# Gate table by adding DMAs, without a one-hot stage, and 96 blocks of the first expert product computed ahead and kept in DRAM

## The chip, the core and the metric

The kernel runs on one core of a Trainium2 chip. The metric is device time in microseconds (us) for one execution. The engines are TensorE (PE; PEld is its weight load), VectorE (DVE), ScalarE (ACT), GpSimd (POOL) and SyncE (SP). SP and ACT issue plain DMAs; GpSimd issues the indirect ones, whose addresses come from a list of indices in SBUF. All of them run on the core's 16 DMA engines.

## The reference

One layer of an encoder serves 512 prompt tokens and 128 sample tokens. Everything up to the last sub-layer (projection, gating, two attentions, delta rule, output projection, norms) is untouched by the change, except that zeros are written to DRAM meanwhile. The last sub-layer retrieves experts by product keys:

```python
q = (h @ w_query).reshape(n, PEER_HEADS, 2, PEER_DQ // 2)
s = jnp.einsum('nhpd,hpkd->nhpk', q, sub_keys, preferred_element_type=jnp.float32)
top_s, top_i = lax.top_k(s, PEER_TOPK)
cand = top_s[:, :, 0, :, None] + top_s[:, :, 1, None, :]
best_s, best_c = lax.top_k(cand.reshape(n, PEER_HEADS, PEER_TOPK * PEER_TOPK), PEER_TOPK)
...
ids = (i1 * PEER_NKEYS + i2).reshape(n, PEER_HEADS * PEER_TOPK)
gates = jax.nn.softmax(best_s, axis=-1).reshape(n, PEER_HEADS * PEER_TOPK)
act = jax.nn.gelu(jnp.einsum('nkd,nd->nk', expert_u[ids], h))
return jnp.einsum('nk,nkd->nd', (gates * act).astype(h.dtype), expert_v[ids])
```

There are 8 heads, 128 keys in each half, 16 picks per head, so 128 (expert, gate) pairs per token out of 128 x 128 = 16384 experts of width 1024.

## The kernel before, in words

Tokens are handled in five tiles of 128 (tiles 0 to 3 prompt, 4 sample). Tiles 0 to 2 (384 tokens, `ND`) take the dense way: for each of 128 blocks of 128 experts the first product (`u_block`, 24 matmuls: high and low parts of a split float32, 8 depth slices) gives 128 experts x 384 tokens, GELU (`u_gelu`) follows, the result is multiplied by a dense table of gates (`g_hi`), split again, and the second product (`v_bank`, 18 matmuls in six accumulators) adds it to the output. Tiles 3 and 4 take the sparse way: for each of their 128 picks, `tick` has GpSimd gather 128 rows of 4 KB of `u` or of `v` by index, and `consume` has VectorE make a dot product (pass 0) or a scaled accumulation (pass 1); that is 2 tiles x 2 passes x 128 = 512 gathers of 512 KB, with six row buffers.

The order of the stages is this. `d_prompt` computes queries and scores of the prompt tiles, 16 half heads one after the other; VectorE picks the top 16 of 128 keys (`half`, `top16`) and of the 80 candidate pairs (`best`). `d_sample` computes the scores of the sample tile. `d_decode` turns picks into expert numbers and gates, tile by tile. `table` makes the dense gates: for each token two one-hot rows (first key; second key times gate), 128 x 128 matmuls, evictions into `stg`, and 12 stores of 2 MB to the DRAM table `gdense`. Beside these, `prefill` computes the first 8 (`LEAD`) blocks of the first product. Up to here a scheduler orders each engine's queue by program order and readiness; `lanes` only interleaves the generators by their yields.

The last loop (`for m in range(NBLK)`, 128 iterations) is ordered by hand: iteration m issues the loads of later blocks on SP (`u_load`, `v_load`, every fourth time `gt_load`, one slice of the gate table), splits block m + 1 of `v` and of the gated activations, splits block m + `LEAD` + 1 of `u`, computes block m + `LEAD` of the first product and block m of the second, and in four places runs `tick` up to `goal(m)`, so that gathers are spread to iteration 118 (`END`). The sample tile's own selection (`sample_select`) lies in iterations 0 to 23. `u_split` and `split` are a cast on ScalarE and a subtraction on VectorE or GpSimd.

Of the kernel before, what the change touches and what calls it, by code (L numbers as in the profile page):

```python
# [14 lines left out]
BF16 = mybir.dt.bfloat16  # L15
# [7 lines left out]
P = 128  # L23
# [5 lines left out]
LEAD = 8  # L29
# [140 lines left out]
def body(tc, I, O):  # L170
# [498 lines left out]
    for i, job in enumerate(jobs):  # L669
        fetch(i + 2)  # L670
        w = ready[i]
# [633 lines left out]
    i1f = T(gq, [P, 4, P], "i1f")  # L1305
    i2f = T(gq, [P, 4, P], "i2f")
    iob = T(gq, [P, 16, 8], "iob", BF16)
    dx = ExitStack()
    qp = pool(dx, "qp", bufs=2, side="right")
    keysT = T(qp, [P, 16, P], "keysT", bufs=1)  # L1310
    V.tensor_copy(out=iob, in_=C("iota")[:, 0:16].unsqueeze(2).to_broadcast([P, 16, 8]))
    LOW = -3.0e38
# [10 lines left out]
    class Select:  # L1323
# [17 lines left out]
        def best(self, h):  # L1341
# [3 lines left out]
            V.tensor_copy(out=self.tib[:, :, :, :, h], in_=self.ti)  # L1345
            cand = T(self.p, [P, nt, 80], "cand", bufs=1)
# [6 lines left out]
            for t in range(nt):  # L1353
                top16(self.p, self.bs[:, t, h, :], self.bc[:, t, h, :], cand[:, t, :], 80, "rest2")
                yield t
# [43 lines left out]
    sel = Select(qp, 4, lambda: T(qp, [P, 16, 16, 8], "eq", BF16, bufs=1))  # L1399
# [12 lines left out]
    def d_prompt():  # L1412
# [28 lines left out]
        for j in range(17):  # L1441
# [12 lines left out]
            if pend is not None:  # L1454
                scores(*pend)
                yield 0.9
# [52 lines left out]
    def d_decode():  # L1509
        for t in range(4):  # L1510
            for cost in sel.decode(t, gates[:, t, :], i1f[:, t, :], i2f[:, t, :]):
                yield 7 if cost is None else 0
        V.scalar_tensor_tensor(out=i1f[:, 3, :], in0=i1f[:, 3, :], scalar=128.0, in1=i2f[:, 3, :], op0=ALU.mult, op1=ALU.add)
        V.tensor_copy(out=idq, in_=i1f[:, 3, :])

    idq = T(gq, [P, P], "idq", U32)

# [14 lines left out]
    def u_block(n):  # L1532

        u = uhs.pop(n)
        gas[n] = T(eu, [P, ND], "ga", bufs=LEAD + 1)
# [7 lines left out]

    def u_gelu(n, pa):
        S.activation(gas[n], pa[:, 0:ND], AF.Gelu_apprx_tanh)

    uls, uhs, gas = {}, {}, {}

    def prefill():
        uls[0] = u_load(0)  # L1550
        uls[1] = u_load(1)
        uhs[0] = u_split(uls.pop(0), G)
        yield 0
        for n in range(LEAD):
            uls[n + 2] = u_load(n + 2)
            uhs[n + 1] = u_split(uls.pop(n + 1), G)
# [9 lines left out]
    gd_ = T(dp, [NG, P, 12, 4, 32], "gdense")  # L1566
    gts = {}

    def gt_load(g):
        gts[g] = T(ep, [P, 12, 4, 32], "gt2") if g % 2 else T(rw, [P, 12, 4, 32], "gt")  # L1570
        nc.sync.dma_start(out=gts[g], in_=gd_[g])

    tx = ExitStack()
    tp = pool(tx, "tp", bufs=2, side="right")

    iob8 = T(tp, [P, P, 8], "iob8", BF16, bufs=1)
    V.tensor_copy(out=iob8, in_=C("iota").unsqueeze(2).to_broadcast([P, P, 8]))

    POOLS = (6, 5, 6, 5)

    def table():
        for t in range(3):
            pt = bank("tp")
            for k, src in enumerate((i1f, i2f, gates)):
                transpose(pt[:, k * P:(k + 1) * P], src[:, t, :])
            sm = T(tp, [P, 2, P], "slots")
            i1b = T(tp, [P, P], "i1b", BF16)
            S.copy(out=i1b, in_=pt[:, 0:P])
            S.copy(out=sm.rearrange("p k t -> p (k t)"), in_=pt[:, P:384])
            iot = C("iota").unsqueeze(1).to_broadcast([P, 8, P])  # L1590

            def slot(k, c, n):
                return sm[:, k, c:c + n].unsqueeze(2).to_broadcast([P, n, P])

            for c in range(4):
                stg = T(tp, [P, P, 32], "stg")
                for n0 in range(0, 32, 8):
                    col = 32 * c + n0
                    ob = T(tp, [P, P, 8], "ob", BF16, bufs=2)
                    o1 = T(tp, [P, 8, P], "o1", bufs=3)  # L1600
                    o2 = T(tp, [P, 8, P], "o2", bufs=3)
                    V.tensor_tensor(out=ob, in0=iob8, in1=i1b[:, col:col + 8].unsqueeze(1).to_broadcast([P, P, 8]), op=ALU.is_equal)  # L1602
                    obn = ob.rearrange("p e n -> p n e")
                    m = POOLS[(col // 8) % 4]
                    G.tensor_tensor(out=o1[:, 0:m, :], in0=obn[:, 0:m, :], in1=slot(1, col, m), op=ALU.mult)  # L1605
                    for n in range(m, 8):
                        S.activation(o1[:, n, :], obn[:, n, :], AF.Copy, scale=sm[:, 1, col + n:col + n + 1])
                    V.tensor_tensor(out=o2, in0=iot, in1=slot(0, col, 8), op=ALU.is_equal)
                    for q in range(0, 8, 4):
# [263 lines left out]
```

## Time and profile before

| what | value |
|---|---|
| three runs | 2171.67, 2174.33 and 2174.74 us, median 2174.33 |
| the profiled execution | 2175.44 us |
| its span, first to last instruction | 2173.7 us |
| mean granted TensorE clock | 0.958 |
| instructions | 32417 |
| DMA traffic | 575.8 MB, of it 268.47 MB by GpSimd's gathers |

The profile counts an engine as busy while an instruction runs on it; durations overlap at their ends, so the distance from start to start is the better price of an instruction in a row of its like. "Idle before" is the time an engine stood still ahead of an instruction, with what released it; "issue" means that nothing in the profile released it. PEclk is the granted clock as a share of the full 2.4 GHz. DMA is the mean busy share of the 16 DMA engines.

### The profile page before, as it was taken

Reading aid. Unit: us, or ns where it says so; the run is one execution under the profiler, and the core shown is the slowest. Engines: PE = TensorE matmul, PEld = TensorE weight load, DVE = VectorE, ACT = ScalarE, POOL = GpSimd, SP = SyncE. Lnnn points to the kernel's source line nnn. Section 1 sums busy time; section 2 is a strip of 40 time slices with the busy share of each in tenths; the row PEclk is TensorE's granted clock in tenths of the full one; section 3 lists DMA queues with packets and bytes.
Section 4 is the critical chain, followed back from the end, with each engine's and each line's share of the span. In section 5 each row is a group of like instructions: output and inputs, shape, how many; then the busy total and the mean of one; then the engine's idle time right before and its main releaser. Section 6 shows DMA issues by size and latency. Waiting matters only on the chain.

```text
span 2173.7 us, 32417 instructions
## 1 busy us (share of the span) xinstructions
PE 1914.0 (88%) x11971; PEld 1603.3 (74%) x11971; DVE 1795.8 (83%) x3883; ACT 726.1 (33%) x1220; POOL 935.3 (43%) x693
## 2 busy tenths in 40 slices
PE   5889899999889887767779999999999999999983
PEld 3889766645667776656668888888888888888862
DVE  5762367766478999968999999999999999999987
ACT  3322133312332338862233333333333332333320
POOL 1322221101312248742346666665666665565610
PEclk8999999999999999998899999999999999999996
DMA  7212242166663436566779999999999999999961
GB/s 273 111 44 79 103 143 103 40 237 227 254 217 137 157 105 181 168 191 243 249 276 409 409 390 390 398 398 398 395 410 405 380 407 383 398 386 404 388 244 68
DMA packets 200248, 575.80 MB, mean 265 GB/s; under 512 B 20463, under 2 KB 73199, under 8 KB 195226
## 3 DMA queue, kind: packets, MB, share of 16 engines
q1 hardware_dynamic: 117978, 295.59, 37.2%
q0 software_dynamic: 73728, 268.47, 31.8%
q10 hardware_dynamic: 8384, 9.68, 1.3%
q8 instruction: 94, 1.54, 0.3%
q14 instruction: 64, 0.52, 0.1%
HBM read 538.79 MB, written 34.36 MB: 264 GB/s over the span
## 4 chain that ended last, share of the span: by engine, by line
issue 17%; POOL 16%; DVE 14%; DMA 5%; ACT 2%; PE 1%; POOLq 0%; ACTq 0%; DVEq 0%
POOL acc L1653 8%; POOL rows L1653 8%; DVE ycs L1668 2%; ACT uh L243 2%; DVE vl L1698 1%; DVE rows L1662 1%; DVE acc L1668 1%; DVE acc L1662 1%; DMA acc<-in_v_dram,idq 1%; DVE ul L244 1%; DMA acc<-in_v_dram,ids 1%; DVE ga L1702 1%; DMA rows<-in_v_dram,idq 1%; DVE wl L1708 1%; DMA acc<-in_u_dram,ids 1%
## 5 line engine op out<-in xcount | busy, mean ns | idle before, releaser
L1705 ACT CAST wh<-ga 128x384 fp32r<-128x384 f32 x128 | 65.7, 514 | 764.0 <-DVE ga L1702 764.0
L188 PE MATMUL mm<-h2h,uh 128*128 128x384 f32 x1024 | 213.8, 350 | 46.6 <-ACT uh L243 45.7
L188 PEld LDWEIGHTS mm<-h2h,uh 128*128 128x128 f32 x1024 | 183.8, 194 | 73.2 <-ACT uh L243 66.3
L188 PE MATMUL mm<-h2l,uh 128*128 128x384 f32 x1024 | 204.6, 341 | 0.0
L188 PE MATMUL mm<-h2h,ul 128*128 128x384 f32 x1024 | 200.6, 336 | 0.0
L188 PE MATMUL sa<-vl,wh 128*128 128x512 f32 x384 | 161.5, 421 | 28.0 <-DVE vl L1698 28.0
L188 PEld LDWEIGHTS mm<-h2l,uh 128*128 128x128 f32 x1024 | 184.2, 193 | 0.0
L188 PE MATMUL sa<-vh,wh 128*128 128x512 f32 x384 | 153.7, 400 | 33.7 <-ACT wh L1705 30.0
L244 DVE TENSOR_TENSOR ul<-ur,uh 128x1024 fp32r<-128x1024 f32 x119 | 145.8, 1226 | 44.2 <-ACT uh L243 44.0
L188 PEld LDWEIGHTS mm<-h2h,ul 128*128 128x128 f32 x1024 | 180.5, 189 | 0.0
L1698 DVE TENSOR_TENSOR vl<-vr,vh 128x1024 fp32r<-128x1024 f32 x128 | 156.1, 1219 | 20.8 <-ACT vh L1695 20.8
L188 PE MATMUL sa<-vh,wl 128*128 128x512 f32 x384 | 152.3, 397 | 0.0
L188 PE MATMUL sa<-o,o 128*128 128x128 f32 x768 | 109.1, 292 | 47.4 <-ACT stg L1613 27.6
L1695 ACT CAST vh<-vr 128x1024 fp32r<-128x1024 f32 x128 | 133.3, 1041 | 39.1 <-DVE vr L1693 21.5
L188 PEld LDWEIGHTS sa<-o,o 128*128 128x128 f32 x768 | 95.8, 198 | 60.8 <-ACT stg L1613 33.5
L243 ACT CAST uh<-ur 128x1024 fp32r<-128x1024 f32 x128 | 134.0, 1047 | 6.9 <-PE mm L188 5.4
L1605 POOL TENSOR_TENSOR o<-ob,slots 128x768 f32<-128x768 bf16 (+1 forms) x48 | 114.5, 2392 | 32.1 <-DVE ob L1602 28.5
L1653 POOL DMA_INDIRECT acc<-in_u_dram,idq x65 | 80.1, 1232 | 109.0 <-DVE gates L1662 101.7
L188 PEld LDWEIGHTS sa<-vl,wh 128*128 128x128 f32 x384 | 73.4, 191 | 67.9 <-DVE vl L1698 54.9
L1653 POOL DMA_INDIRECT rows<-in_u_dram,idq x63 | 80.4, 1277 | 72.4 <-DVE gates L1662 67.1
L244 POOL TENSOR_TENSOR wlo<-raw,whi 128x2048 fp32r<-128x2048 f32 (+1 forms) x12 | 55.2, 4603 | 126.1 <-ACT whi L243 123.3
L188 PEld LDWEIGHTS sa<-vh,wh 128*128 128x128 f32 x384 | 73.1, 190 | 47.6 <-ACT wh L1705 32.6
(482 smaller groups left out, 4849.0 us busy)
## 6 DMA issues: line engine op xcount, KB each, us to landing
ur<-in_uT_dram SPq DMA_DIRECT2D x128, 512.0 KB
vr<-in_v_dram SPq DMA_DIRECT2D x128, 512.0 KB
gt<-gdense SPq DMA_DIRECT2D x32, 768.0 KB
gdense<-stg SPq DMA_DIRECT2D x11, 2048.0 KB
wada<-in_wada_dram SPq DMA_DIRECT2D x16, 1024.0 KB
acc<-in_ckT_dram SPq DMA_DIRECT2D x32, 512.0 KB
cv<-in_cv_dram SPq DMA_DIRECT2D x32, 512.0 KB
wqr<-in_wq_dram SPq DMA_DIRECT2D x32, 512.0 KB
```

Of the source, the lines that this page charges most:

```text
L188: PE.matmul(out, lhsT=lhsT, rhs=rhs, start=start, stop=stop, **kw)
L243: S.copy(out=hi, in_=raw)
L244: e_lo.tensor_tensor(out=lo, in0=raw, in1=hi.bitcast(F32), op=ALU.subtract)
L1605: G.tensor_tensor(out=o1[:, 0:m, :], in0=obn[:, 0:m, :], in1=slot(1, col, m), op=ALU.mult)
L1653: G.indirect_dma_start(out=r, out_offset=None, in_=I["v"] if k else I["u"], in_offset=bass.IndirectOffsetOnAxis(ap=who[t][0][:, s:s + 1], ...
L1662: V.tensor_tensor_reduce(out=r, in0=r, in1=h2, scale=1.0, scalar=0.0, op0=ALU.mult, op1=ALU.add, accum_out=act[:, s:s + 1])
L1668: V.scalar_tensor_tensor(out=facc[t], in0=r, scalar=act[:, s:s + 1], in1=facc[t], op0=ALU.mult, op1=ALU.add)
L1695: S.copy(out=vs[n][0], in_=w)
L1698: V.tensor_tensor(out=vs[n][1], in0=vls.pop(n), in1=vs[n][0].bitcast(F32), op=ALU.subtract)
L1702: V.tensor_tensor(out=ga.rearrange("p (c n) -> p c n", c=12), in0=ga.rearrange("p (c n) -> p c n", c=12), in1=gts[n // 4][:, :, n % 4, :], ...
L1705: S.copy(out=ws[n][0], in_=ga)
L1708: V.tensor_tensor(out=ws[n][1], in0=gas.pop(n), in1=ws[n][0].bitcast(F32), op=ALU.subtract)
```

## The change

The one-hot stage goes. Instead the gates are placed by address. In the early projection stage SP writes zeros over a DRAM table `gsc` of 128 x 128 x 384 floats, in 16 DMAs. `SelectHead.best` decodes each head as soon as its picks are known, for four tiles at once, and computes for tiles 0 to 2 the flat address expert x 384 + token in `idx`. `add_gates` then issues, for one tile and one of the 128 picks, an indirect DMA of 128 single floats that adds the gates to the table; 3 x 128 = 384 of them. They are issued by GpSimd: nine after each half head's scores, three at a time in `d_add` beside the sample's scores, the rest in a new loop. Adds of the same tile and different heads may meet at one element and are ordered; all others are declared free of each other.

The new loop, ordered by hand, computes blocks 5 to 95 (`FIRST`) of the first product alone; `prefill` does blocks 0 to 4. Their GELUs go to the DRAM tensor `gad` by ACT's queue. In it run the remaining adds, 170 (`EARLY_ROWS`) of the 512 gathers, and one step of `sample_select` per block; an add with no gather behind it is followed by a one-element memset. The last loop reads the blocks below 96 back (`ga_load`), and computes first-product blocks only from iteration 90 on; `LEAD` is 6, the loads run three blocks ahead, and the table slices are read from `gsc`. The low parts of the first blocks of `u` are made by VectorE instead of GpSimd.

```diff
-LEAD = 8
+LEAD = 6
+FIRST = 96
...
+    gsc = T(dp, [P * P * ND, 1], "gsc")
+    zero = T(rg, [P, 768], "zero", bufs=1)
+    G.memset(zero, 0.0)
+    def gates_zero(i):
+        a = P * ND // 16
+        nc.sync.dma_start(out=gsc.rearrange("(p x) one -> p (x one)", p=P)[:, i * a:(i + 1) * a].rearrange("p (r z) -> p r z", z=768),
+                          in_=zero.unsqueeze(1).to_broadcast([P, a // 768, 768]))
...
+        for k in range(2 if i in (1, 2, 3, 4, 5, 6, 7, 8) else 0):
+            gates_zero(2 * (i - 1) + k)
...
+    class SelectHead(Select):
+        def __init__(self, pl):
+            self.p, self.nt = pl, 4
+        def best(self, h):
+            pl, tv = self.p, self.tv
+            tib = T(pl, [P, 16, 2, 4], "tib", BF16)
+            V.tensor_copy(out=tib.rearrange("p n k t -> p t k n"), in_=self.ti)
+            bs = T(pl, [P, 4, 16], "bs")
...
+            hs = slice(16 * h, 16 * h + 16)
+            e = T(pl, [P, 4, 16], "e")
+            V.tensor_tensor(out=e, in0=bs, in1=bs[:, :, 0:1].to_broadcast([P, 4, 16]), op=ALU.subtract)
+            S.activation(e, e, AF.Exp)
...
+            ku = T(pl, [P, 4, 16], "ku", U32)
+            V.tensor_scalar(out=ku, in0=bc, scalar1=3, scalar2=None, op0=ALU.logical_shift_right)
+            kf, pf, y = (T(pl, [P, 4, 16], n) for n in ("kf", "pf", "yk"))
...
+            eq = T(pl, [P, 16, 16, 8], "eq", BF16, bufs=1)
+            V.tensor_tensor(out=eq, in0=ab_.unsqueeze(2).to_broadcast([P, 16, 16, 8]),
+                            in1=iob.unsqueeze(1).to_broadcast([P, 16, 16, 8]), op=ALU.is_equal)
+            V.tensor_tensor(out=eq, in0=eq, in1=tib.rearrange("p n k t -> p n (k t)").unsqueeze(1).to_broadcast([P, 16, 16, 8]), op=ALU.mult)
+            for n in (8, 4, 2):
+                V.tensor_tensor(out=eq[:, :, 0:n, :], in0=eq[:, :, 0:n, :], in1=eq[:, :, n:2 * n, :], op=ALU.add)
+            i12 = T(pl, [P, 16, 8], "i12")
+            V.tensor_tensor(out=i12, in0=eq[:, :, 0, :], in1=eq[:, :, 1, :], op=ALU.add)
+            ids_ = T(pl, [P, 4, 16], "idf")
+            i12v = i12.rearrange("p s (k t) -> p k t s", k=2)
+            V.scalar_tensor_tensor(out=ids_, in0=i12v[:, 0], scalar=128.0, in1=i12v[:, 1], op0=ALU.mult, op1=ALU.add)
+            V.tensor_copy(out=idq[:, hs], in_=ids_[:, 3, :])
+            V.scalar_tensor_tensor(out=idx[:, :, hs], in0=ids_[:, 0:3, :], scalar=float(ND),
+                                   in1=pnt.unsqueeze(2).to_broadcast([P, 3, 16]), op0=ALU.mult, op1=ALU.add)
+            to_add.extend((t, h, r) for t in range(3) for r in range(16))
+            yield
...
+    sel = SelectHead(qp)
+    to_add = []
+    def add_gates(n):
+        for _ in range(min(n, len(to_add))):
+            t, h, r = to_add.pop(0)
+            c = 16 * h + r
+            ins = G.indirect_dma_start(out=gsc, out_offset=bass.IndirectOffsetOnAxis(ap=idx[:, t, c:c + 1], axis=0),
+                                       in_=gates[:, t, c:c + 1], in_offset=None, compute_op=ALU.add).ins
+            for key in [f"add{t}_{h}"] + [f"add{u}" for u in range(3) if u != t]:
+                tc.declare_no_dep(ins, group=key, reason="no element in common")
+            for key in (f"add{t}_{h}", f"add{t}"):
+                tc.add_to_no_dep_group(key, ins)
...
                 scores(*pend)
+                add_gates(9)
...
-    def d_decode():
-        for t in range(4):
-            for cost in sel.decode(t, gates[:, t, :], i1f[:, t, :], i2f[:, t, :]):
-                yield 7 if cost is None else 0
...
+    gad = T(dp, [FIRST, P, ND], "gad")
...
+            S.activation(fresh[n], pa[:, 0:ND], AF.Gelu_apprx_tanh)
+            nc.scalar.dma_start(out=gad[n], in_=fresh.pop(n))
...
+    EARLIEST = 5
...
+        for n in range(EARLIEST):
+            uls[n + 3] = u_load(n + 3)
+            uhs[n + 1] = u_split(uls.pop(n + 1), V)
             u_gelu(n, u_block(n))
-            yield 5
-    gen_u = prefill()
-    lanes((d_sample(), 0, 1.0), (d_decode(), 0, 1.0), (itertools.islice(gen_u, 3), 0, 1.0))
+            yield 6
...
+    def d_add():
+        while to_add:
+            add_gates(3)
+            yield 1.9
+    lanes((d_sample(), 0, 1.0), (prefill(), 0, 1.0), (itertools.islice(d_add(), 16), 0, 1.0))
...
-    def table():
-        for t in range(3):
...
+        nc.sync.dma_start(out=gts[g], in_=gsc.rearrange("(g b e n) one -> g e b (n one)", b=4, e=P, n=ND)[g])
...
+    def ga_load(n):
+        if n < FIRST:
+            gas[n] = T(ep, [P, ND], "gr", bufs=3)
+            nc.sync.dma_start(out=gas[n], in_=gad[n])
+    EARLY_ROWS = 170
 
     def goal(m):
-        cost = lambda n: 2 * min(n, NBLK - LEAD) + max(0, n - (NBLK - LEAD))
-        return int(len(work) * min(1.0, cost(m + 1) / cost(END)))
+        cost = lambda n: n + max(0, n - (FIRST - LEAD)) - max(0, n - (NBLK - LEAD))
+        return EARLY_ROWS + int((len(work) - EARLY_ROWS) * min(1.0, cost(m + 1) / cost(END)))
...
+    for n in range(EARLIEST, FIRST):
+        left = FIRST - 3 - n
+        k = n - EARLIEST
+        to = EARLY_ROWS * (k + 1) // (FIRST - EARLIEST)
+        if n + 3 < NBLK:
+            uls[n + 3] = u_load(n + 3)
+        if n == FIRST - 2:
+            for b in range(2):
+                v_load(b)
+                ga_load(b)
+        quota = -(-len(to_add) // left) if left > 0 else len(to_add)
+        for q in range(quota):
+            add_gates(1)
+            if at[0] < to:
+                tick(at[0] + 1)
+            else:
+                G.memset(spare, 0.0)
+            if q == 0:
+                uhs[n + 1] = u_split(uls.pop(n + 1), V)
+        if not quota:
+            uhs[n + 1] = u_split(uls.pop(n + 1), V)
+        tick(to)
+        u_gelu(n, u_block(n))
+        for _ in itertools.islice(ssel, 1):
+            pass
+    for _ in ssel:
+        pass
+    gt_load(0)
+    v_load(2)
+    ga_load(2)
...
+    FIN = NBLK - LEAD - 1
     for m in range(NBLK):
-        n = m + LEAD
-        g0 = goal(m - 1) if m else 0
+        n = m + LEAD if m + LEAD >= FIRST else NBLK
+        g0 = goal(m - 1) if m else EARLY_ROWS
         part = lambda j: tick(g0 + (goal(m) - g0) * j // 4)
-        if n + 2 < NBLK:
-            uls[n + 2] = u_load(n + 2)
-        if m + 2 < NBLK:
-            v_load(m + 2)
+        if n + 3 < NBLK:
+            uls[n + 3] = u_load(n + 3)
+        if m + 3 < NBLK:
+            v_load(m + 3)
+            ga_load(m + 3)
...
```

## Rows read from the trace of the kernel before

**Rows 1.** The page: busy time by engine; DMA share in 40 slices.
```profile
PE 1914.0 (88%) x11971; PEld 1603.3 (74%) x11971; DVE 1795.8 (83%) x3883; ACT 726.1 (33%) x1220; POOL 935.3 (43%) x693
...
DMA  7212242166663436566779999999999999999961
```

**Rows 2.** Windows: us, busy of each engine (instructions), granted clock, DMA share, GB/s.
```profile
560.00:751.00 191.00, 172.89 (x1243) 138.95 (x1234) 150.37 (x898) 58.51 (x96) 49.07 (x24) 0.97 0.53 191
751.00:803.00 52.00, 45.18 (x301) 42.44 (x300) 50.56 (x120) 18.20 (x42) 12.96 (x5) 0.93 0.35 122
803.00:965.00 162.00, 114.55 (x802) 101.17 (x801) 155.97 (x96) 140.39 (x220) 124.58 (x55) 0.97 0.57 163
965.00:1126.00 161.00, 111.04 (x480) 97.41 (x479) 135.02 (x381) 36.12 (x50) 48.22 (x41) 0.86 0.73 251
1126.00:2068.00 942.00, 907.12 (x4462) 792.70 (x4462) 892.71 (x1102) 298.68 (x430) 579.46 (x460) 1.00 1.01 396
2068.00:2174.00 106.00, 64.09 (x243) 49.66 (x241) 88.04 (x168) 16.89 (x24) 7.44 (x6) 0.77 0.41 148
```

**Rows 3.** Timeline of TensorE, one iteration: start, us, instruction, count.
```profile
1241.08 0.40 PE L188 MATMUL sa<-vh,wh 128*128 128x512 f32 x1
...
1245.22 1.55 PE L188 MATMUL mm<-h2h,uh 128*128 128x384 f32 x8
...
1249.38 0.40 PE L188 MATMUL sa<-vh,wh 128*128 128x512 f32 x1
```

**Rows 4.** Timeline of VectorE, same iteration and a later one; [idle before].
```profile
1238.59 1.22 DVE L1662 CUSTOM_DVE_ANT_0 acc<-acc,h2q 128x1024 f32<-128x1024 f32 x1
...
1239.74 0.55 DVE L1702 TENSOR_TENSOR ga<-ga,gt 128x384 f32<-128x384 f32 x1
1241.36 0.08 DVE L1662 DVE_READ_ACCUMULATOR2_ANT gates<- 128x1 f32 x1
1241.82 1.23 DVE L244 TENSOR_TENSOR ul<-ur,uh 128x1024 fp32r<-128x1024 f32 x1 [0.39 <-ACT uh L243]
...
1482.84 1.23 DVE L244 TENSOR_TENSOR ul<-ur,uh 128x1024 fp32r<-128x1024 f32 x1 [0.32 <-ACT uh L243]
```

**Rows 5.** The page's costliest groups: busy, mean ns, idle before: the one-hot rows.
```profile
L1605 POOL TENSOR_TENSOR o<-ob,slots 128x768 f32<-128x768 bf16 (+1 forms) x48 | 114.5, 2392 | 32.1 <-DVE ob L1602 28.5
```

**Rows 6.** Groups by shape; one source line (min/median/max ns, first, last start).
```profile
L1316 DVE MAX8 tv<-sc 128x8 f32<-128x128 f32 x64 | 16.8, 281 | 32.8 <-ACT sc L1425 32.8
...
L244 POOL TENSOR_TENSOR wql<-wqr,wqh 128x1024 fp32r<-128x1024 f32 x16 | 38.3, 2394 | 102.4 <-PE mm L188 57.3 <-ACT wqh L243 30.7 <-PE sa L188 14.4
...
L1345 DVE CAST tib<-ti x8: 447/453/457, 595.6 to 748.2; 128x128 bf16<-128x128 uint32 x8
```

**Rows 7.** GpSimd's gathers: the source line's forms, then four instructions of its timeline.
```profile
L1653 POOLq EVENT_SEMAPHORE  x503: 17/17/43, 798.2 to 2076.7; - x168
L1653 POOL DMA_INDIRECT acc<-in_u_dram,idq x65: 937/1015/1967, 802.7 to 1290.3; - x65
...
817.80 1.25 POOL L1653 DMA_INDIRECT acc<-in_u_dram,idq  x1 [0.16 <-issue]
...
1238.94 1.68 POOL L1653 DMA_INDIRECT acc<-in_u_dram,idq  x1 [0.60 <-DVE gates L1662]
1240.93 1.31 POOL L1653 DMA_INDIRECT acc<-in_u_dram,idq  x1 [0.30 <-issue]
...
1482.51 0.94 POOL L1653 DMA_INDIRECT rows<-in_v_dram,idq  x1 [0.30 <-issue]
```

**Rows 8.** DMA: GpSimd's queue (packets, MB, share); a window of the one-hot stage.
```profile
q0 software_dynamic: 73728, 268.47, 31.8%
...
850.00:950.00 100.00, 72.19 (x510) 62.91 (x509) 100.00 (x62) 90.25 (x143) 76.24 (x32) 0.99 0.60 169
```

**Rows 9.** SP's first table load; the gate product's source line.
```profile
967.22 3.32 SPq L1571 DMA_DIRECT2D gt<-gdense  x1
...
L1702 DVE TENSOR_TENSOR ga<-ga,gt x128: 536/552/558, 980.9 to 2139.4; 128x384 f32<-128x384 f32 x128
```

More of the change, by code (lines that the diff above doesn't have):

```diff
@@ L1311, in body @@
     V.tensor_copy(out=iob, in_=C("iota")[:, 0:16].unsqueeze(2).to_broadcast([P, 16, 8]))
+    V.tensor_tensor(out=act_s, in0=C("iota"), in1=ident, op=ALU.mult)
+    V.tensor_reduce(out=pnt[:, 0:1], in_=act_s, axis=AX.X, op=ALU.add)
+    for t in (1, 2):
+        V.tensor_scalar(out=pnt[:, t:t + 1], in0=pnt[:, 0:1], scalar1=float(P * t), scalar2=None, op0=ALU.add)
     LOW = -3.0e38
@@ L1345, in best, with sums @@
             V.tensor_copy(out=self.tib[:, :, :, :, h], in_=self.ti)
+            cand = self.sums(tv)
+            for t in range(nt):
+                top16(self.p, self.bs[:, t, h, :], self.bc[:, t, h, :], cand[:, t, :], 80, "rest2")
+                yield t
+        def sums(self, tv):
+            nt = self.nt
             cand = T(self.p, [P, nt, 80], "cand", bufs=1)
@@ L1352, in best @@
                             in1=tv[:, :, 1, 0:8].unsqueeze(2).to_broadcast([P, nt, 7, 8]), op=ALU.add)
-            for t in range(nt):
-                top16(self.p, self.bs[:, t, h, :], self.bc[:, t, h, :], cand[:, t, :], 80, "rest2")
-                yield t
+            return cand
         def decode(self, t, gate_o, i1_o, i2_o):
@@ L1579, in body @@
-    POOLS = (6, 5, 6, 5)
-    def table():
-        for t in range(3):
[L1583 to L1609, printed above, removed]
-                        pg = bank("sa")
-                        for n in range(4):
-                            mm(pg[:, n * P:(n + 1) * P], o2[:, q + n, :], o1[:, q + n, :])
-                        S.copy(out=stg[:, :, n0 + q:n0 + q + 4].rearrange("p i n -> p n i"), in_=pg.rearrange("p (n i) -> p n i", n=4))
-                    yield 1
-                for g0, g1 in ((0, 4), (4, NG)) if t == 2 and c == 3 else ((0, NG),):
-                    nc.sync.dma_start(out=gd_[g0:g1, :, 4 * t + c].rearrange("g e i n -> e g (i n)"),
-                                      in_=stg[:, 4 * g0:4 * g1, :].rearrange("p (g i) n -> p g (i n)", g=g1 - g0))
-                    if g1 == 4:
-                        gt_load(0)
@@ L1629, in body @@
     ep = pool(ex, "ep", side="right")
-    gs, act_s, act_q, gs_q = (gates[:, k, :] for k in range(4))
+    gs_q = gates[:, 3, :]
     ids = T(ep, [P, P], "ids", U32)
@@ L1820, in body @@
             u_gelu(n, pa)
-        if m < 24:
-            for _ in itertools.islice(ssel, 3):
-                pass
-        if m == NBLK - LEAD:
+        if m == FIN:
             final_rows()
@@ L1830, in body @@
                 consume()
-        if m == NBLK - LEAD + 1:
+        if m == FIN + 1:
             base(3)
@@ L1835, in body @@
             x_get(0)
-        if m == NBLK - LEAD + 2:
+        if m == FIN + 2:
             base(4)
@@ L1841, in body @@
             final(3)
-        if m == NBLK - LEAD + 3:
+        if m == FIN + 3:
             final(4)
```

70 lines of the change are left out of this document (40 added, 30 removed).

## The prediction

> **What bounds the kernel now.** I read three things in order: the page's busy shares, a table of stretches, then the instructions of one iteration on each engine. The shares [rows 1] name no single bound: TensorE 88%, VectorE 83%, GpSimd 43%, and the DMA line is full only in the second half. The table [rows 2] shows why. From 560 to 803 us VectorE picks the top 16 (busy 150 of 191 us, then 51 of 52). From 803 to 965 us the one-hot stage fills VectorE (156 of 162). From 965 to 1126 us the second product's first 12 blocks run beside the sample rows' selection, and VectorE (135 of 161) sets the pace. From 1126 to 2068 us TensorE (907 of 942), VectorE (893) and the DMA engines (share 1.01, 396 GB/s) are full together. Then come 106 us of tail.
>
> One iteration of the full stretch [rows 3]: a first-product block is three runs of 8 matmuls, 1245.22 to 1249.38, 4.16 us; a second-product block is the 18 matmuls before it, 1241.08 to 1245.22, 4.14 us. The next iteration begins 8.30 us after the last, so with four gathered rows TensorE is the bound. VectorE starts one 1024-wide instruction every 1.15 us and loses 0.39 us on ScalarE's cast [rows 4]; with five rows it is the bound. DMA is a near third: 2 x 512 KB of weights, 192 KB of gate table, 4.3 rows of 512 KB.
>
> **What goes.** The whole one-hot stage, 162 us [rows 2]: 48 groups with 114.5 us of GpSimd [rows 5], nearly all VectorE time, 768 products of 128 columns, 25 MB of table written in 512-byte runs. The first-product blocks computed there (six of LEAD) are not lost, only moved.
>
> **What comes.** (a) Decoding per head instead of per tile. Eight wide multiplies over 2048 elements before (four tiles, two halves), eight after (one per head holds both halves of four tiles): the same wide work. Twelve short operations per head at about 0.15 us replace fourteen per tile at about 0.2 (estimates from their start pitch): 8 x 12 x 0.15 = 14 us against 11, and with the index sums I take 9 us more. The splits of six blocks move from GpSimd to VectorE: 6 x 1.15 = 7 us. VectorE idled 32.8 us waiting for scores [rows 6], which could swallow part of it. The first gather started at 802.7 [rows 7]; I put the early loop's start at 818, between 803 (all swallowed) and 835 (short decode operations wait for GpSimd).
>
> (b) 25 MB of zeros on SP's queue among the projection's weights, 16 x 1.57 MB. At 396 GB/s that is 63 us of DMA time, where the DMA line stands at 1 to 4 tenths [rows 1]. Each fetch is issued ahead of its zeros and is needed a job later. I cost it at nothing; without that cover it is at most 20 us.
>
> (c) 96 blocks stored and read back: 2 x 18.9 MB, 95 us at 400 GB/s, paid below. ScalarE issues the stores behind its own GELU and has two thirds of its time free.
>
> (d) 384 adding DMAs, each 128 single elements, all issued by GpSimd. This decides. No row shows one; the nearest is the row gather, also 128 descriptors: its minimum is 937 ns and its maximum 1967 [rows 7], and q0 has 144 packets for each of the 512 [rows 8]. Its length hangs on VectorE: the gather at 1482.51, with VectorE between instructions, took 0.94 us; those at 1238.94 and 1240.93 took 1.68 and 1.31 and both ended (1240.62, 1242.24) 0.88 us after a VectorE instruction began or ended (1239.74, 1241.36) [rows 4, 7]. So a gather waits out the running VectorE instruction, then needs 0.88 us. The Trainium skill, SBUF — State Buffer, section on two separate sides, says that GpSimd cannot write descriptors while VectorE holds the port pair they share; that trace agrees, 0.94 against 1.68 us. By its account the adds in the early loop would stretch as the gathers did. Between gathers lie 0.30 us of issue, or 0.16 behind other work [rows 7]; 503 of 512 gathers have a semaphore instruction, which most adds would not need. So one add is 0.94 + 0.16 = 1.10 us at the least and 1.61 at the most usual back-to-back pace of gathers. I take 1.20, near the low end, because the selection's VectorE instructions are short (281 ns [rows 6]). A gather between adds: 1.24 to 1.61, I take 1.45.
>
> **The chain of GpSimd.** Adds can begin when the first head is decoded: its cast is at 595.6 us [rows 6], plus 11 us, 607 (an estimate: 20 short instructions like MAX8's and the per-head decode). From then on GpSimd holds 384 adds x 1.20 = 461, ten splits of query weights x 2.4 = 24 [rows 6], and in the early loop 165 of its 170 gathers x 1.45 = 239 and some 36 one-element memsets, 5 us. 607 + 461 + 24 + 239 + 5 = **1336 us**. Of these adds 135 run in the prompt's selection (nine per half head from the second on, 10.8 us plus 2.4 against VectorE's some 13), 48 beside the sample's scores, 201 in the early loop. The rest of the early loop is shorter: TensorE 4.16 us a block; DMA 0.52 + 0.20 + 1.87 x 0.52 = 1.70 MB, 4.25 us at 400 GB/s; VectorE 1.15 + 0.39 + 1.87 x 1.15 = 3.7. GpSimd needs 2.2 x 1.20 + 1.87 x 1.45 = 5.4. The gates' waits name what queues behind them: an add waits for the same tile's adds of the head before, 32 adds earlier, and behind it stand the gathers, and VectorE and so TensorE wait for those.
>
> **Behind the early loop.** The first table slice waits for the last add; before, 13.7 us passed from its issue at 967.22 to the first gate product at 980.9 [rows 9]. I take 12. Then 90 iterations with the second product alone: TensorE 4.14, VectorE 1.15 + 2 x 0.47 + 2.34 x 1.15 = 4.8, DMA (0.524 weights + 0.197 read back + 0.197 table + 2.34 x 0.524 = 2.15 MB) 5.36 at 400 GB/s: **482**. Then 28 iterations with both, 3.70 MB, 9.25 us: **259** (VectorE 2 x 1.15 + 0.94 + 0.39 + 4.68 x 1.15 = 9.0). The tail was 106 us from 2068 [rows 2], where iteration 117 begins; two more first-product blocks lie in it: 106 + 8 = **114**.
>
> Sum: 1336 + 12 + 482 + 259 + 114 = 2203. The profiled execution took 2175.4 us with a span of 2173.7, so 1.7 lie around it: **2205 us**. That execution is 1.1 above the median 2174.3, within the runs' spread. So I forecast slower by 1.4%: the 162 us of the one-hot stage are more than spent, since GpSimd ends the early loop at 1336 where TensorE alone would end it near 818 + 91 x 4.16 = 1197, and splitting the two products costs the stores and loads of (c).
>
> **Rivals.** *Adds are cheap to issue: faster.* If an add holds GpSimd for less than 0.93 us, the early loop is bound by TensorE and DMA: 818 + 91 x 4.25 = 1205, plus 28 for the sample's selection (48 us of VectorE against 0.57 spare in each of 30 blocks), 1233 us, and the time 2102. For it: an add moves 512 bytes, a gather 512 KB, and the 0.94 us may hold a part that goes with bytes. Against it: descriptors are as many. No change lies at an end of the loop at 1306 us, an add of 1.12 us: the low end of my price already crosses it.
>
> *The adds clog the DMA engines: slower still.* One mechanism, in the early loop: each element is a read and a write in DRAM of four bytes, and eight per engine stand ahead of the next rows. From 512-byte runs at share 0.60 and 169 GB/s (29 ns each) [rows 8] and 4 KB rows at 396 GB/s (165 ns) [rows 2] a run has about 10 ns of its own; three passes are 30 ns, 0.24 us per add and engine. It decides from 0.49 us per add: (485 - 387) / 201, GpSimd's time in the loop (201 x 1.20 + 239 + 5, begun at 607 + 183 x 1.20 + 24 = 851) less the loop's other DMA time. At 1.6 us, 0.2 us an element, the loop takes 387 + 322 = 709 and the time is 2429. The Trainium skill, DMA: Bandwidth & Descriptors, Specifications, says that transfers under 512 bytes become read-modify-writes, which speaks against 49,152 transfers of 4; no row here shows the price of one.
>
> *It repays itself exactly: no change.* An add at 1.11 to 1.13 us. TensorE's lower share in either loop (some 76%) is a smaller risk on the same side as mine: between 965 and 1126 us, busy 111 of 161, the granted clock was 0.86 [rows 2].
>
> **How the numbers follow.** GpSimd chain, 0.50: with 1.10 and 1.24 us it ends at 1263 and the time is 2132; with 1.40 and 1.61, 1440 and 2309. Of the 0.50, 0.38 is slower, 0.06 within 0.2% (about what a measurement of this kernel can tell from no change), 0.06 faster. Cheap adds, 0.33, all faster. Clogged DMA, 0.14, and 0.03 for other losses, all slower. Faster 0.39, same 0.06, slower 0.55. The range 2105 to 2310 leaves out the lower part of the cheap case (0.12) and the clogged one beyond it (0.08); the likeliest case alone spans 2132 to 2309.
>
> **What would show it.** Right: GpSimd nearly gapless from about 610 us until the last add, at 5 us or more per early block; the last add near 1330; TensorE idle in that loop behind VectorE, which waits for gathered rows; 5.3 to 5.5 us per block after it. Wrong: early blocks of 4.2 to 4.4 us with idle GpSimd (cheap adds); gathers that land late while GpSimd idles (clogged DMA); the second product's blocks well under 5.3 us (DMA faster than 400 GB/s).

## The result and the profile after

The changed kernel takes 2575.4 us (median of four, 2561.4 to 2582.2) against 2173.1 for the kernel before: 1.184 times as long, 95% interval 1.179 to 1.189. The forecast was 2205, in a range up to 2310. The direction was right, the size was not: 370 us are missing from the sum. The profiled execution took 2574.3 us with a span of 2572.6 and a mean granted clock of 0.879 (0.958 before).

The page of the changed kernel: busy time by engine, the DMA share in 40 slices, GpSimd's queue, and the group of the adds (busy, mean ns, idle before).

```profile
PE 1927.1 (75%) x11194; PEld 1602.0 (62%) x11194; DVE 1648.3 (64%) x3861; ACT 607.4 (24%) x1000; POOL 1441.1 (56%) x1058
...
DMA  7860531766324247777888888899999999999971
...
q0 software_dynamic: 129024, 268.69, 34.7%
...
L1489 POOL DMA_INDIRECT gsc<-gates,idx x384 | 656.8, 1711 | 116.1 <-issue 107.7
```

Against [rows 1] every engine's share has fallen but GpSimd's. Its queue has 55,296 more packets than in [rows 8], 144 for each add, as for each gather.

The stretches that answer to [rows 2], cut where the stages now end (us, busy of PE, PEld, DVE, ACT, POOL, granted clock, DMA share, GB/s):

```profile
615.00:980.00 365.00, 148.74 (x941) 115.99 (x940) 153.51 (x868) 40.01 (x82) 310.78 (x192) 0.71 0.39 66
980.00:1031.00 51.00, 48.23 (x289) 46.78 (x289) 28.55 (x102) 19.83 (x33) 26.20 (x23) 0.93 0.76 241
1031.00:1668.00 637.00, 445.31 (x2082) 424.88 (x2082) 338.99 (x595) 136.63 (x177) 532.73 (x380) 0.87 0.82 229
1668.00:2208.00 540.00, 439.17 (x1658) 337.56 (x1657) 445.13 (x612) 144.07 (x191) 264.78 (x219) 0.88 0.98 369
2208.00:2467.00 259.00, 242.40 (x1181) 209.11 (x1180) 246.50 (x248) 76.67 (x111) 172.40 (x129) 1.00 1.02 398
2467.00:2573.00 106.00, 59.12 (x248) 48.21 (x246) 82.07 (x162) 16.76 (x24) 2.80 (x2) 0.79 0.35 129
```

From the first add (614.8) to the last (started at 1666.7, ended at 1669.3) GpSimd is busy 311 of 365 us and 533 of 637; the rest is the 0.30 us ahead of each DMA. No other engine reaches half of that first stretch. The prompt's selection, which ended at 751 before, lasts until 980. There TensorE waits for a GpSimd split (five times, the longest 55.9 us) that stands behind a row of adds:

```profile
PE mm L189 <- POOL wql L245: 157.0, 5, 55.9
```

The adds themselves: their source line (min/median/max ns, first and last start) with its semaphore instructions, three adds while TensorE and VectorE waited, and a piece of the early loop where they alternate with gathers and memsets.

```profile
L1489 POOL DMA_INDIRECT gsc<-gates,idx x384: 1546/1572/2622, 614.8 to 1666.7; - x192
L1489 POOLq EVENT_SEMAPHORE  x4: 17/17/17, 693.7 to 1000.3; - x4
```

```profile
640.63 1.55 POOL L1489 DMA_INDIRECT gsc<-gates,idx  x1 [0.30 <-issue]
642.49 1.56 POOL L1489 DMA_INDIRECT gsc<-gates,idx  x1 [0.30 <-issue]
644.35 1.55 POOL L1489 DMA_INDIRECT gsc<-gates,idx  x1 [0.30 <-issue]
...
1103.90 0.99 POOL L1702 DMA_INDIRECT rows<-in_u_dram,idq  x1 [0.30 <-issue]
1105.20 1.57 POOL L1489 DMA_INDIRECT gsc<-gates,idx  x1 [0.30 <-issue]
1106.19 0.62 POOL L1851 MEMSET spare<- 1x1 f32 x1
1107.08 1.73 POOL L1489 DMA_INDIRECT gsc<-gates,idx  x1 [0.27 <-issue]
```

An add never takes less than 1.546 us, where the gather of [rows 7] has a minimum of 0.937, and the next one starts 1.86 us after it with nothing else running. That is above the highest price that the forecast names (1.61). The gathers beside it still take 0.99. The memset starts inside the add before it and costs almost nothing.

### The profile page after: what moved, and what is told of

Its sections match the earlier page's. It is cut to its first block, busy times and chain, and to the rows that moved or that the text cites. A ratio compares the mean times of both kernels' runs of the same rounds, so it can differ in the third digit from the quotient of the medians.

```text
span 2572.6 us, 31482 instructions
## 1 busy us (share of the span) xinstructions
PE 1927.1 (75%) x11194; PEld 1602.0 (62%) x11194; DVE 1648.3 (64%) x3861; ACT 607.4 (24%) x1000; POOL 1441.1 (56%) x1058
## 3 DMA queue, kind: packets, MB, share of 16 engines
q0 software_dynamic: 129024, 268.69, 34.7%
## 4 chain that ended last, share of the span: by engine, by line
POOL 30%; issue 19%; PE 19%; DVE 15%; DMA 15%; ACT 1%; SPq 0%; ACTq 0%; POOLq 0%; DVEq 0%
POOL gsc L1489 16%; PE mm L189 9%; POOL rows L1702 7%; POOL acc L1702 6%; DMA gt<-gsc 5%; PE a L189 3%; PE g L189 2%; DMA rows<-in_u_dram,idq 2%; DMA acc<-in_u_dram,idq 2%; PE sa L189 2%; DVE ycs L1717 1%; DVE acc L1717 1%; DVE vl L1747 1%; DMA gsc<-gates,idx 1%; POOL wql L245 1%
## 5 line engine op out<-in xcount | busy, mean ns | idle before, releaser
L1489 POOL DMA_INDIRECT gsc<-gates,idx x384 | 656.8, 1711 | 116.1 <-issue 107.7
L189 PE MATMUL mm<-h2h,ul 128*128 128x384 f32 x1024 | 240.2, 383 | 187.4 <-DVE ul L245 187.3
L189 PEld LDWEIGHTS mm<-h2h,ul 128*128 128x128 f32 x1024 | 204.1, 216 | 207.8 <-DVE ul L245 207.6
L189 PEld LDWEIGHTS mm<-h2h,uh 128*128 128x128 f32 x1024 | 211.3, 220 | 28.1 <-ACT uh L244 26.2
L189 PE MATMUL mm<-h2h,wql 128*128 128x512 f32 (+1 forms) x144 | 41.2, 438 | 157.0 <-POOL wql L245 157.0
L1639 ACT ACTIVATE ga<-mm 128x384 f32<-128x384 f32 x96 | 47.2, 492 | 453.4 <-PE mm L189 433.3
L1711 DVE CUSTOM_DVE_ANT_0 rows<-rows,h2q 128x1024 f32<-128x1024 f32 x63 | 77.2, 1226 | 119.0 <-DMA rows<-in_u_dram,idq 118.9
L1711 DVE CUSTOM_DVE_ANT_0 acc<-acc,h2q 128x1024 f32<-128x1024 f32 x65 | 79.6, 1225 | 106.8 <-DMA acc<-in_u_dram,idq 105.2
L1753 ACT CAST wh<-gr 128x384 fp32r<-128x384 f32 x96 | 49.3, 513 | 357.6 <-DVE gr L1751 357.5
L189 PEld LDWEIGHTS mm<-h2h,wql 128*128 128x128 f32 x144 | 30.0, 226 | 165.4 <-POOL wql L245 159.2
```

Source lines behind the costliest of these rows:

```text
L189: PE.matmul(out, lhsT=lhsT, rhs=rhs, start=start, stop=stop, **kw)
L1489: ins = G.indirect_dma_start(out=gsc, out_offset=bass.IndirectOffsetOnAxis(ap=idx[:, t, c:c + 1], axis=0), in_=gates[:, t, c:c + 1], in_of ...
L1639: S.activation(fresh[n], pa[:, 0:ND], AF.Gelu_apprx_tanh)
L1711: V.tensor_tensor_reduce(out=r, in0=r, in1=h2, scale=1.0, scalar=0.0, op0=ALU.mult, op1=ALU.add, accum_out=act[:, s:s + 1])
L1753: S.copy(out=ws[n][0], in_=ga)
```

## The experiments

**Four kinds of indirect DMA side by side.** In the place of each four adds stand one add, one plain store, one gather of single elements and one add of 16 elements:

```diff
+            kind = r % 4
...
+            if kind == 0:
+                ins = G.indirect_dma_start(out=gsc, out_offset=off, in_=gates[:, t, c:c + 1], in_offset=None, compute_op=ALU.add).ins
+            elif kind == 1:
+                ins = G.indirect_dma_start(out=gput, out_offset=off, in_=gates[:, t, c:c + 1], in_offset=None).ins
+            elif kind == 2:
+                ins = G.indirect_dma_start(out=got[:, 32 * t + c // 4:32 * t + c // 4 + 1], out_offset=None, in_=uflat, in_offset=off).ins
+            else:
+                ins = G.indirect_dma_start(out=gpart, out_offset=off16, in_=gates[0:16, t, c:c + 1], in_offset=None, compute_op=ALU.add).ins
```

> Prices of four kinds of indirect DMA side by side, one after the other in the place of the adds: (0) the adding one as it is, 128 elements; (1) a plain store of 128 elements without adding, to another table; (2) a gather of 128 single elements; (3) an adding one of 16 elements only. So three quarters of the gates are missing from the table. If adding makes the price: (0) 1.55 us, (1) and (2) 0.94. If single elements make it: 1.55 for (0), (1) and (2). If the direction to DRAM makes it: (0) and (1) 1.55, (2) 0.94. If GpSimd pays per descriptor, (3) is 0.2 to 0.5 us; if per instruction, (3) is 1.5. With (3) cheap and the others unchanged the time is near 2450 us.

The four source lines of that kernel:

```profile
L1497 POOL DMA_INDIRECT gsc<-gates,idx x96: 1572/1589/2660, 611.6 to 1537.2; - x96
...
L1499 POOL DMA_INDIRECT gput<-gates,idx x96: 982/992/2033, 613.7 to 1540.3; - x96
...
L1501 POOL DMA_INDIRECT got<-in_u_dram,idx x96: 956/1004/2126, 615.0 to 1543.8; - x96
...
L1503 POOL DMA_INDIRECT gpart<-gates,idx x96: 1340/1370/2373, 616.3 to 1546.8; - x96
```

Adding makes the price: 1.59 us against 0.99 and 1.00 (medians). Neither the size of the elements nor the direction matters. An eighth of the elements takes only 0.22 off, so most of it is paid per instruction. Packets don't set it either: in GpSimd's queue a gather of rows has 144 of them like an add, and takes 0.99 us; an add of 16 elements and a plain store have 32 each (12,288 packets for 384, in two kernels below), and take 1.37 and 0.99. The time of the one execution was 2446.2 us. That it lies near the 2450 expected is luck: not one cheap kind but three made it, 96 x (0.60 + 0.59 + 0.22) = 135 us less than the changed kernel.

**No adds; half of the adds.** The call is left out, or left out for odd picks:

```diff
-            ins = G.indirect_dma_start(out=gsc, ..., compute_op=ALU.add).ins
...
```

> The 384 adding DMAs are not issued, so the gates never reach the table; everything else of the change stays (zeros, per-head decode, 96 blocks to DRAM and back). Theory (the adds' time on GpSimd is what was lost): GpSimd has left 170 gathers of 1.48 us and the memsets, TensorE and DMA bound the early loop, it begins near 820 and ends at 1210 to 1240 us, and the time is 2100 to 2150 us. Rival (what costs is the rest: storing and reading back 96 blocks, two loops instead of one): the time stays above 2300 us.

2115.1 us, 0.972 of the kernel before (0.970 to 0.974). The early loop of that kernel runs at the pace of TensorE (busy 353 of 367 us) and DMA (share 1.01) together, as the rival of cheap adds had it:

```profile
845.00:1212.00 367.00, 352.73 (x2000) 345.70 (x1998) 322.18 (x560) 131.55 (x171) 225.48 (x186) 1.00 1.01 387
```

```diff
+            if r % 2:
+                continue
```

> Every second adding DMA is left out (192 of 384), so half of the gates are missing from the table. Theory (GpSimd works without a gap from the first add to the last, at 1.96 us from add to add): 192 x 1.96 = 376 us off its chain, the last add at 1290 to 1320 us, time 2200 to 2240 us. Rival (the loss is in the prompt's selection, where the splits of the query weights stand behind adds and TensorE waits 157 us for them): the selection gets shorter by up to 80 us and the early loop keeps its pace of 7.3 us per block, time near 2490 us.

2274.6 us (1.046, 1.044 to 1.047), 301 less than with all of them but 35 to 75 above what I expected. GpSimd had a pause that I hadn't counted (what it waited for; us, times, longest):

```profile
POOL acc L1704 <- DVE tv L1335: 81.6, 1, 81.6
```

After its share of adds it issues six gathers ahead; the seventh waits for a row buffer, which VectorE frees only in the early loop, and that loop stands behind the selection in VectorE's queue. In the changed kernel the same pause is 19.8 us.

**Table slices in runs of 6 KB.** Before the change a partition's slice was one run of 6144 bytes; in the new table it is four of 1536.

```diff
-... gsc.rearrange("(g b e n) one -> g e b (n one)", ...)
+... gsc.rearrange("(g e b n) one -> g e b (n one)", ...)
```

> Only the address pattern of the table slices' reads is changed: each partition reads one run of 6144 bytes instead of four of 1536, so the gates arrive at other experts. Theory A (short runs make the slices slow, VectorE waits 90 us for them in the stage with the second product alone): that stage goes from 5.9 to 5.4 us an iteration, time 2525 to 2540 us. Theory B (the DMA engines are full in that stage and the slice is only what is waited for last): less than 10 us, 2565 to 2575 us.

2530.1 us, 45 less. In the stage with the second product alone VectorE's waits for a slice fall from 90.5 to 31.2 us (first the changed kernel, then this one) and DMA moves 404 instead of 369 GB/s:

```profile
DVE gr L1751 <- DMA gt<-gsc: 90.5, 22, 6.1
...
DVE gr L1751 <- DMA gt<-gsc: 31.2, 23, 2.8
...
1668.00:2160.00 492.00, 413.56 (x1655) 315.24 (x1656) 448.26 (x613) 146.93 (x192) 262.37 (x218) 0.96 1.03 404
```

**Storing instead of adding; 16 elements instead of 128.**

```diff
-... in_offset=None, compute_op=ALU.add).ins
+... in_offset=None).ins
```

> All 384 DMAs store instead of adding (the compute operation is left out); addresses, counts and waits stay, so where a token meets an expert twice one gate is lost. Theory (GpSimd's time per adding instruction is the loss): 0.99 instead of 1.58 us each, 0.59 x 384 = 227 us off GpSimd's chain, last store near 1440 us, time 2330 to 2370 us. Rival (the DMA engines are clogged by 49152 four-byte elements, whether stored or added): the time stays above 2500 us.

2439.2 us (1.122, 1.119 to 1.126): 136 less, where I expected 205 to 245. The stores took 0.97 us, and the last started at 1538. Without waits, stores and memsets took 532 us from start to start where adds and memsets took 766, about the 227 us less that were expected. But GpSimd lost 95 of them again by waiting: the pause shown above was 80.1 us, at 930 us, instead of 19.8, and five waits for ScalarE and VectorE ahead of it, of 4 to 15 us, sum to 35.

```diff
-... ap=idx[:, t, c:c + 1] ... in_=gates[:, t, c:c + 1] ...
+... ap=idx[0:16, t, c:c + 1] ... in_=gates[0:16, t, c:c + 1] ...
```

> Each of the 384 adding DMAs takes 16 elements instead of 128, so seven eighths of the gates are missing; the number of instructions and their waits stay. Theory (GpSimd pays per instruction): 1.37 instead of 1.58 us each, 0.2 x 384 = 77 us less, last add near 1590 us, time 2480 to 2510 us. Rival (the elements clog the DMA engines, at 0.44 to 0.52 us of all 16 engines per add): seven eighths of that go, and the time falls to 2115 to 2200 us, as without adds.

2474.5 us (2467.8 to 2499.0), 101 less: a little more than the chain of GpSimd gives, far from what a DMA bound would. The elements do cost DMA time: GpSimd's queue took 34.7% of 2572.6 us in the changed kernel and 32.7% of 2121.2 without adds, 199 us more (892.7 less 693.6), 0.52 us of all 16 engines per add. The queue without adds, and with plain stores:

```profile
q0 software_dynamic: 73728, 268.47, 32.7%
...
q0 software_dynamic: 86016, 268.69, 31.1%
```

The 0.52 is an estimate that takes the gathers' packets as equally long in both traces; the kernels with half and with a third of the adds give 0.44 to 0.51 by the same sum.

**More stores ahead of the early loop.** This is the kernel with stores, with one number changed:

```diff
-... itertools.islice(d_add(), 16) ...
+... itertools.islice(d_add(), 40) ...
```

> As the run in which all 384 DMAs store instead of adding (so a token's second meeting of an expert overwrites the first), but 120 instead of 48 of them are handed out beside the sample's scores. In that run GpSimd stood still for 80 us at 930 us: the stages before had used up their stores, and the seventh gather waited for a row buffer that VectorE freed late. Theory (that pause kept the saving from reaching the time): the pause goes, last store near 1460 us, time 2350 to 2380 us. Rival (past some 2440 us another resource, DMA or VectorE, sets the early loop): within 15 us of 2439.

2457.8 us: no gain, so my reading of the pause was incomplete. The pause was still there (88.4 us, from 1010 us on). While GpSimd issued stores 1.26 us apart, TensorE issued one instruction every 2 to 3 us and waited for nothing that the profile shows, from 890 us on:

```profile
926.38 0.48 PE L189 MATMUL mm<-h2l,uh 128*128 128x384 f32 x1 [2.32 <-issue]
```

From 890 to 990 us the DMA engines moved 0.54 MB. With plain stores TensorE has 58.3 us of such waits between 615 and 930; with adds it has less than 1 us. What holds the other engines there is open.

**The weights' splits on VectorE.**

```diff
-        split(w, hi, lo, G)
+        split(w, hi, lo, V)
```

> The low parts of the query weights are made by VectorE instead of GpSimd, nothing else is changed. Theory (one chain of GpSimd work from the first add to the last): only the ten splits of 3.2 us that lie between adds leave it, 32 us, time 2535 to 2550 us, although the selection itself gets shorter by over 100 us. Rival (the loss is made in the selection, where TensorE waits 157 us for those splits): all of that comes back, time 2420 us or less.

2531.2 us: 44 less. The selection does get its time back (the first block's GELU starts at 785 instead of 983 us), but the last add moves only from 1667 to 1624. That is what GpSimd's chain gives: 28 us of splits and the 19.8 us pause go, the first add comes 7 us earlier, and adds and gathers take 12 us longer. Of TensorE's 157 us of waiting the rest was never on the path.

**A third of the adds, in bunches and evenly.**

```diff
+            if t:
+                continue
```

> Only the 128 adds of tile 0 are issued, so two thirds of the gates are missing. Theory (an add costs time only where GpSimd has none free): GpSimd's work no longer sets the early loop, the adds there cost some 0.5 us of DMA time each, 67 x 0.5 = 34 us over the 2115 us without adds: 2140 to 2170 us. Rival (each add costs the same wherever it stands, 460 us / 384 = 1.2 us): 2115 + 128 x 1.2 = 2270 us.

2221.6 us (1.020, 1.017 to 1.023): between the two expectations. The kernel below keeps that edit and changes the order:

```diff
-to_add.extend((t, h, r) for t in range(3) for r in range(16))
+to_add.extend((t, h, r) for r in range(16) for t in range(3))
```

> Again only the 128 adds of tile 0, two thirds of the gates missing, but now handed out evenly (the three tiles in turn) instead of in runs of 16 with 32 left out behind them. Theory (an add costs time only in a block in which GpSimd has more to do than TensorE; in the run before, the blocks with two adds were as slow as those of the changed kernel and the ones without were at TensorE's pace): the early loop gives back 30 to 50 of its 65 us, time 2165 to 2190 us. Rival (the adds cost their own time whatever stands beside them): as before, 2215 to 2225 us.

2174.2 us (0.999, 0.998 to 1.001): the same 128 adds for 47 us less. One stretch of either early loop, first bunched, then even:

```profile
950.00:1025.00 75.00, 58.31 (x282) 54.78 (x281) 60.23 (x153) 21.32 (x27) 60.12 (x49) 0.89 0.89 265
```

```profile
950.00:1025.00 75.00, 66.42 (x367) 62.91 (x366) 69.23 (x143) 26.12 (x34) 63.98 (x47) 1.00 0.99 333
```

Evenly spread they cost (2174.2 - 2115.1) / 128 = 0.46 us each, about their DMA time; the last 192 of the 384 cost (2575.4 - 2274.6) / 192 = 1.57.

**Could adds replace a third of the one-hot stage?** The experiments point to a kernel between the two: the kernel before, with tile 0 by adds (beside the selection) and tiles 1 and 2 by one-hot rows.

```diff
+    tab0 = T(dp, [NG * P * 512, 1], "tab0")
...
-        for t in range(3):
+        for t in (1, 2):
...
-                    G.tensor_tensor(out=o1[:, 0:m, :], ...)
+                    (G if late else V).tensor_tensor(out=o1[:, 0:m, :], ...)
```

> The kernel before, with tile 0's gates placed by 128 adding DMAs while GpSimd has time during the selection, and only tiles 1 and 2 through the one-hot stage (zeros for a third of the table, decode per head, query weights' low parts and five of the first blocks' on VectorE; in the first 18 of 32 one-hot groups VectorE multiplies in GpSimd's place). If the adds hide behind the selection: 162/3 = 54 us less one-hot, 18 x 0.86 = 15 us for the multiplications and 10 us for the splits on VectorE: 2140 to 2160 us. If the heads' adds, which must follow one another, hold GpSimd past 900 us and the one-hot groups wait for it: 2165 to 2200 us.

2221.9 us (1.021, 1.018 to 1.023). Neither case as written: SP's first read of the new table was queued ahead of the weights of the sample's scores and waited for the last add.

```profile
889.98 3.78 PE L188 MATMUL sa<-h2T,wqr 128*128 128x128 f32 x16 [64.84 <-DMA wqr<-in_wq_dram]
```

```diff
+        if g:
+            gt_adds(g)
...
     v_load(0)
+    gt_adds(0)
```

> As the kernel with tile 0 by adds and tiles 1 and 2 through the one-hot stage, but the first read of the table that the adds write is issued after the one-hot stage. In that kernel it stood in SP's queue at 825 us, waited for the last add until 886 us, and behind it the weights of the sample's scores and of the first blocks. If that queue made the loss: 60 us come back, 2150 to 2170 us, a little faster than the kernel before. If GpSimd's adds hold the stage by themselves (they end at 883 us): 2195 us or more.

2189.6 us (1.006, 1.005 to 1.008). 32 came back; then a split of the first product behind the adds held ScalarE and TensorE 50 us:

```profile
PE mm L188 <- POOL ul L244: 50.4, 1, 50.4
```

```diff
-            uhs[n + 1] = u_split(uls.pop(n + 1), V if n < 4 else G)
+            uhs[n + 1] = u_split(uls.pop(n + 1), V)
```

> As the run before it (tile 0 by adds, tiles 1 and 2 by the one-hot stage, the first read of the adds' table issued late), with the low parts of the remaining blocks of the first product on VectorE too. In that run ScalarE's cast and TensorE stood 51 us, from 849 to 900 us, for one such split that lay behind the last adds in GpSimd's queue. If that wait is the loss: 2189 less 50, plus 4 x 1.2 us of VectorE: 2140 to 2160 us, faster than the kernel before. If the stage then waits for the adds elsewhere: 2180 us or more.

2173.7 us (0.9985, 0.9967 to 1.0003): no difference from the kernel before, and neither case as written. In the profiled execution the one-hot groups' own GpSimd part waits behind the adds (46.5 us), because of this:

```profile
843.27 2.90 POOL L1499 DMA_INDIRECT tab<-gates,idx  x1 [0.30 <-issue]
846.47 40.79 POOL L1499 DMA_INDIRECT tab<-gates,idx  x1 [0.31 <-issue]
887.57 4.35 POOL L1499 DMA_INDIRECT tab<-gates,idx  x1 [0.30 <-issue]
892.22 1.55 POOL L1499 DMA_INDIRECT tab<-gates,idx  x1 [0.31 <-issue]
```

```profile
845.00:885.00 40.00, 36.10 (x267) 32.65 (x268) 40.00 (x40) 38.87 (x64) 39.69 (x2) 1.00 0.63 175
```

From 845 to 885 us VectorE ran 40 tensor-tensor instructions without a gap, and one add took 40.79 us. That execution was the slowest of twelve (2186.0 us), and the longest add in any other trace took 5.26 us, so how often such a wait comes is not shown. Nor is why this add was passed over so long: in the same gapless row, from 834 to 846 us, four adds took 2.65 to 2.91.

**The sample's selection spread thin.**

```diff
-        if m == 24:
+        if m == 36:
...
-        if m < 24:
-            for _ in itertools.islice(ssel, 3):
+        if m < 36:
+            for _ in itertools.islice(ssel, 1):
```

> The kernel before, with the sample rows' own selection spread over iterations 0 to 30 of the last loop at one step each instead of three steps each in the first ten; the gates' final rows are built at iteration 36 instead of 24. It asks whether the stretch from 965 to 1126 us, where VectorE is full and DMA moves 251 GB/s, can give back some of its 60 us of unused DMA time. If VectorE's slack of later iterations takes the work: 2140 to 2160 us. If VectorE is as full there (893 of 942 us): within 10 us of the kernel before.

2170.3 us (0.9984, 0.9972 to 0.9996), some 3 us less. From 965 to 1126 us DMA now moves 329 instead of 251 GB/s, from 1126 to 2068 us 386 instead of 396: what one stretch gains, the other mostly pays, and the loop is full as a whole. No version beats the kernel before by a margin worth having.

## Why the prediction was wrong, step by step

| term | forecast, us | measured, us |
|---|---|---|
| end of the last add (measured: the cut above) | 1336 | 1668 |
| first slice, 90 iterations | 12 + 482 | 540 |
| 28 iterations with both products | 259 | 259 |
| tail | 114 | 106 |

**The chain of GpSimd** was the right mechanism: GpSimd works nearly without a gap until the last add, the early loop waits for it, and taking adds away shortens it. That the change is slower came out for the reason forecast. Up to the last add 163 gathers took 241 us from start to start, 1.48 each against the 1.45 taken; the first add came 8 us late, and nine splits took 28 us against 24 for ten.

**The step that failed is the price of one add**, "0.94 + 0.16 = 1.10 us at the least and 1.61 at the most usual back-to-back pace of gathers", and the 1.20 between them. It was taken from the gather because both have 128 descriptors. Equal counts of packets held (144 each), equal time did not: adding takes 0.6 us more per instruction, and no row of the kernel before shows a DMA that adds. A smaller part of the same term failed too. The 0.16 us of issue was for DMAs without a semaphore instruction; only 4 of the 384 adds have one, and nearly each (361) still stood behind 0.30 us of issue. From start to start the 384 adds with their 37 memsets took 786 us, of which 19.8 are the pause: 766 / 384 = 1.99 each, 300 us over the 466 of the sum. With the pause that is 320 of the 332 that are missing there. The range could not hold this. Its upper end, 2309, went with 1.40 us an add, below the 1.61 of the same paragraph, and both were prices of another operation, so neither was a bound.

**Waiting for VectorE** was read rightly and is a small part: some 0.15 us per add (1.99 less 1.55 and 0.30), where the sum had 0.10 in its 1.20. The trace of the kernel before bears the reading out: all 115 gathers that start while VectorE makes the low part of `v` (a tensor-tensor instruction, in most cases with 0.87 us left) take 1.67 us or more, and the 95 that start while VectorE stands take at most 0.95. Where TensorE and VectorE stand, adds come 1.86 us apart; in the early loop 63 of 201 are at least 0.3 us longer than the shortest. The Trainium skill, SBUF — State Buffer, section Who interferes with whom, says that the engine that finds the shared port pair taken blocks fully while the other's instruction lasts. The add of 40.79 us agrees with the blocking, but it stood through 38 of VectorE's instructions, not one. The same section says that tensor-tensor instructions contend with GpSimd's reads and infers that they don't hold up the writing of descriptors. Here only tensor-tensor instructions ran beside the add, and it was held; whether in reading its indices or in writing descriptors is not shown.

**The selection.** "Nine per half head, 10.8 us plus 2.4 against VectorE's some 13" fails by the same price: nine adds take 16.7, so GpSimd set the selection's pace, and the splits queued behind up to 45 adds. It looks like the main loss (157 us of TensorE waiting), but moving the splits gave back 44.

**Clogged DMA** was the rival nearest to a second bound. An add costs some 0.44 to 0.52 us of DMA time, about twice my estimate of 0.24 and near the 0.49 from which it was to decide. That point held for adds of 1.20 us; at 1.99 GpSimd is later than DMA (share 0.82 in that loop). With half of the adds the loop's share is 0.96 (915 to 1371 us), with a third evenly spread 0.99 to 1.03: there DMA time is what an add costs. The Trainium skill, DMA: Bandwidth & Descriptors, Specifications, says that transfers under 512 bytes become read-modify-writes. No run here shows whether plain stores of 4 bytes do; by the same estimate they took (31.1% of 2435.4 less 693.6) / 384 = 0.17 us, so most of the 0.52 comes with the adding.

**Cheap adds** was right about the loop without GpSimd's load, and wrong in its condition: 2102 worked out, 2115 measured without adds. That the two are so close is partly luck. The early loop ended at 1212, 21 us before the 1233 of that sum, and the stage with the second product alone took 529 us instead of 494. The 28 us for the sample's selection in it are 31 by their own terms (48 less 30 x 0.57).

**The stage with the second product alone** cost 46 us more than forecast. I took 400 GB/s and did not count that the change cuts the slices' runs from 6144 to 1536 bytes. With long runs it is 404 GB/s and 45 us less. This was in the diff and not in my sum.

**The rest of the change** was not tried part by part. Without adds the early loop ends at 1212, inside the 1205 to 1233 worked out for it, so zeros and decode together cost no more than forecast. TensorE's granted clock followed its waiting: on average 0.71 and 0.87 of 2.4 GHz in the two stretches in which it stood behind GpSimd's work, 1.00 in the same loop without adds.

## What to carry to other kernels

A price may be borrowed from another operation's row only for what they share; if the new one adds a function (here the sum in DRAM), leave the upper end open, or measure it by itself first. Work that is handed to an idle engine is free only as far as that engine is idle in each stretch, so hand it out evenly, and look what stands behind it in the same in-order queue (46 to 65 us in each of the three kernels with tile 0 by adds). When data is laid out anew, count the length of the runs in which it is read back.

## What the runs showed of the hardware

An adding indirect DMA holds GpSimd 1.55 to 1.59 us, a plain one 0.95 to 1.00, whichever its direction; with 16 elements instead of 128 the adding one takes 1.28 to 1.37. A gather of rows that starts 0.87 us before a VectorE tensor-tensor instruction ends takes 1.68 us instead of 0.94. Beside a gapless row of VectorE instructions an add took 2.65 to 2.91 us, and once 40.79. Plain stores 1.26 us apart slowed the other engines' issue to one TensorE instruction in 2 to 3 us, adds 1.86 us apart did not; why is open.
